# Low parts of the attention stage's weights: a subtraction on VectorE, or a negated copy on ScalarE and an accumulating DMA

## The chip, the core and the metric

The kernel runs on one core of a Trainium2 chip. The core has five instruction streams that run beside each other and meet only through semaphores: TensorE (PE in the profile) multiplies matrices, VectorE (DVE) and ScalarE (ACT) work elementwise, GpSimd (POOL) here clears small tiles and issues some DMAs, and SyncE (SP) issues most DMAs. Each stream executes strictly in its own order: an instruction that waits holds up everything behind it in that stream. The metric is the device time of one execution in microseconds (us); less is better.

## The reference

One layer of a decoder over 1024 tokens of width 1024, batch 1, in float32:

```python
h = rms_norm(x, attn_norm_w)
q, k, v, u, g = split(h @ w_in)                     # w_in: 1024 x 7168
a = rms_norm(diff_attention(q, k, v), subln_w)      # 8 heads, two softmaxes each, causal, shared bias
y_a = a @ w_proj_attn
c = silu(layer_norm(causal_depthwise_conv(u_a * sigmoid(u_b))))   # width 31
y_b = c @ w_proj_conv
g_a, g_b = split(sigmoid(g + gate_b))
x = x + (g_a * y_a + g_b * y_b) @ w_out
h = rms_norm(x, ffn_norm_w)
gt, up = split(h @ w_gate_up)
x = x + (silu(gt) * up) @ w_down
```

The inputs are float32, and the result is to keep close to float32 accuracy.

## The kernel before

TensorE multiplies in a fast format, float32r, which keeps fewer bits of the mantissa. To get the accuracy back, each operand is held as two tiles: a high part (`hi`, the value rounded to float32r) and a low part (`lo`, the value minus its high part). A product is then three matmuls, hi by hi, hi by lo and lo by hi (`mm3`, lines 159 to 162), all added up in one PSUM bank. Weights have to be split on the core, since they arrive from memory as plain float32.

**A weight fetch.** One fetch brings 512 KB of weights as a 128 x 1024 tile `wraw` (DMAs on SP's queue, line 287 in `ld_cols` for one fetch of 128 columns, line 308 in `ld_wide` for 512 rows of 256 columns). `wsplit` (line 276) then makes the two parts. ScalarE copies `wraw` to `whi` with rounding (`split_hi`, line 120), and VectorE subtracts `whi` from `wraw` into `wlo` (`split_lo`, line 125). There are two buffers for `wraw` and three each for `whi` and `wlo`. A `wraw` buffer can be loaded again once its subtraction is done. A `whi` or `wlo` buffer can be written again once the last matmul that reads it is done.

**The stream.** All weight fetches stand in one list (`Stream`, class `ws`). When a piece of work takes its next weights (`next`), the stream first starts new fetches until it holds three. So a fetch is begun while the two before it are still waiting to be used.

**The stages.** First the input norm and the projections of V, U and the first Q/K head, with convolution taps put between them on VectorE. Then attention, which interleaves three kinds of work: the 64 blocks of attention proper (8 heads by 8 row blocks), the rest of the input projection as filler (`later`: 7 Q/K items, 16 gate items, one to five per head), and the convolution taps that are left (`bg`). Then the two output projections, the merge, `w_out`, and the feed-forward layer.

**Attention.** For a head and a row block, `scores` (line 1009) multiplies on TensorE (lines 1022 and 1023, tile `sc`), adds the bias and takes the row extreme on VectorE (line 1024), takes the exponential on ScalarE (line 1029), and combines the two softmaxes on VectorE (line 1038). `turn` transposes the result on TensorE (line 1061, tile `pT`) and splits it into `ph` (ScalarE) and `pl` (VectorE); where a pair of row blocks is begun, POOL clears a corner of both (lines 1051 and 1052). `weigh` multiplies with V (tile `pW`), ScalarE copies the product out (`ar`, line 1075), and `back` transposes it and normalises (tiles `pB`, `an`, `jk`, lines 1081 to 1090). `subln_T` transposes a finished head (`pS`, `at`, lines 1102 to 1110). Filler items write PSUM tiles `pg`, which ScalarE takes out (`qkraw`, lines 756 to 759, for Q/K; `sgg`, line 603, for the gates). A finished Q/K item is transposed (`pQ`, line 774) and its parts are copied across partitions by DMAs on SP's queue (tiles `qs` and `ks`, lines 785 to 796).

**What sets the order.** The program is recorded by a framework that builds each engine's instruction stream from its own estimate of when each instruction would become ready; a few places pin the order by hand (`issue_after`). So an edit in one place changes the order of the streams around it. Waits and semaphores follow from which tiles are read and written.

**What the change touches.** `wsplit` alone, and only while the flag `inatt` is set. The flag is set at the start of attention and cleared after it; until now it only decided when the transposes of Q/K items are recorded. Thirty fetches are begun while it is set: twelve for Q/K heads 2 to 7, sixteen for the gates, and the first two of `w_proj_attn`. The feed-forward stage calls `wsplit` too, but with the flag cleared.

Of the kernel before, what the change touches and what calls it, by code (L numbers as in the profile page):

```python
# [12 lines left out]
AF = mybir.ActivationFunctionType  # L13
ALU = mybir.AluOpType
# [43 lines left out]
def kernel(  # L58
# [28 lines left out]
    dve, act, pool, pe = nc.vector, nc.scalar, nc.gpsimd, nc.tensor  # L87
# [24 lines left out]
    def nm(s):  # L112
        uid[0] += 1
        return f"{s}_{uid[0]}"

    def f32(ap):
        return ap.bitcast(F32)

    def split_hi(dst, src):
        act.copy(dst, src)  # L120
# [3 lines left out]
    def split_lo(dst, src, hi):  # L124
        last_lo[0] = dve.tensor_tensor(dst, src, f32(hi), op=ALU.subtract).ins  # L125
# [147 lines left out]
    def wtiles():  # L273
        return [wp.tile([P, 1024], F32R, tag=t_, name=nm(t_)) for t_ in ("whi", "wlo")]

    def wsplit(raw, tiles=wtiles):
        hi, lo = tiles()
        split_hi(hi[:], raw[:])
        split_lo(lo[:], raw[:], hi[:])
        return hi, lo  # L280

    def ld_cols(w, c0, tiles=wtiles):


        def go():
            raw = wraw()
            nc.sync.dma_start(
                raw[:].rearrange("p (k c) -> p k c", c=P),
                w[:, c0 : c0 + P].rearrange("(k p) c -> p k c", p=P),
            )  # L290
            hi, lo = wsplit(raw, tiles)
            return (
                hi[:].rearrange("p (k c) -> p k c", c=P),
                lo[:].rearrange("p (k c) -> p k c", c=P),
            )

        return [go]

    def ld_wide(w, cols):


        def half(g):
            def go():
                raw = wraw()
                r3 = raw[:].rearrange("p (k c) -> p k c", c=256)
                o = 0
                for c0, n in cols:
                    nc.sync.dma_start(
                        r3[:, :, o : o + n],
                        w[512 * g : 512 * (g + 1), c0 : c0 + n].rearrange(  # L310
                            "(k p) c -> p k c", p=P
                        ),
                    )
                    o += n
                hi, lo = wsplit(raw)
                return (
                    hi[:].rearrange("p (k c) -> p k c", c=256),
                    lo[:].rearrange("p (k c) -> p k c", c=256),
                )

            return go

        return [half(0), half(1)]
# [88 lines left out]
    def ld_pair(w, k, c):  # L412


        def go():
            raw = wraw()
            nc.sync.dma_start(
                raw[:].rearrange("p (k c) -> p k c", c=512),
                w[k * P : (k + 2) * P, 512 * c : 512 * (c + 1)].rearrange("(k p) c -> p k c", p=P),
            )  # L420
            hi, lo = wsplit(raw)
            return hi[:].rearrange("p (k c) -> p k c", c=512), lo[:].rearrange("p (k c) -> p k c", c=512)

        return go
# [378 lines left out]
                late.append((free if h else 0, lambda a_=(z, key, b, raw): turn_qk(*a_)))  # L803
            yield

    inatt = [False]
    MAKE = {"V": v_item, "U": u_item, "Q": q_item, "G": g_item}

    def run(items):
# [970 lines left out]
```

## Time and profile before

| quantity | value |
|---|---|
| median of 3 runs | 1759.88 us (1759.63 to 1760.11) |
| span of the profiled execution | 1756.3 us (no other time is listed for it) |
| median less span | 3.6 us |
| TensorE busy | 1743.5 us, 99% of the span |
| weight loads of TensorE (PEld) | 1501.9 us, 86% |
| VectorE busy | 1269.9 us, 72% |
| ScalarE busy | 807.5 us, 46% |
| GpSimd busy | 28.8 us, 2% |
| granted clock of TensorE | 1.000 |
| memory traffic | 175.55 MB read, 78.16 MB written |

The profile is one execution, taken by the hardware profiler. An engine is "busy" while an instruction executes; a wait is idle time in front of an instruction, put down to whatever released it last. Matmuls overlap their neighbours, so that a matmul's own duration (0.39 us for 512 columns) is longer than the distance to the next one; the distances are what TensorE's time is made of. Attention takes the span from 316 to about 842 us. "Landing" of a DMA is the time from its issue until its data are in place.

### The profile page before, as it was taken

To read this page: it belongs to the slowest core of one execution; us is meant where nothing else is said; L and a number is where in the kernel's file an instruction comes from. 1 tells how busy PE (TensorE), PEld (TensorE's weight loads), DVE (VectorE), ACT (ScalarE), POOL (GpSimd) and SP (SyncE) were. 2 spreads that over 40 slices of the span, in tenths; PEclk is the share of its full clock that TensorE was granted. 3 is DMA by queue.
4 is the path that set the end of the run, shared out by engine and by line. 5 is a ranking of instruction groups with operands and counts; after the bars stand their busy time and mean duration, and the time that the engine had idled before them with its cause. 6 is when DMAs were issued, how large, how long until landed. Compare 5 with 4: busy or idle time off the path is not lost.

```text
span 1756.3 us, 25881 instructions
## 1 busy us (share of the span) xinstructions
PE 1743.5 (99%) x9377; PEld 1501.9 (86%) x9377; DVE 1269.9 (72%) x2168; ACT 807.5 (46%) x1894; POOL 28.8 (2%) x107
## 2 busy tenths in 40 slices
PE   9999999999999999999999999999999999999999
PEld 7898998999998998988787888888888888888887
DVE  7388888998988988977777525876667666565544
ACT  5111341657776776765456313643333333333332
POOL 2001000000000000000000000000000000000000
PEclk9999999999999999999999999999999999999999
DMA  6237353234434444344872544235545544598663
GB/s 208 93 114 221 108 167 109 72 104 132 103 113 132 119 119 122 95 128 141 292 241 99 168 168 144 91 102 164 164 146 168 173 151 144 164 354 291 216 219 129
DMA packets 253156, 271.68 MB, mean 155 GB/s; under 512 B 15666, under 2 KB 177498, under 8 KB 253028
## 3 DMA queue, kind: packets, MB, share of 16 engines
q1 hardware_dynamic: 250848, 263.25, 47.0%
q0 software_dynamic: 1744, 5.19, 1.1%
q8 instruction: 74, 1.21, 0.3%
q10 hardware_dynamic: 436, 1.58, 0.2%
q14 instruction: 54, 0.44, 0.1%
HBM read 175.55 MB, written 78.16 MB: 144 GB/s over the span
## 4 chain that ended last, share of the span: by engine, by line
PE 92%; DMA 3%; DVE 2%; ACT 1%; issue 1%; SPq 0%; ACTq 0%; DVEq 0%
PE acc L1626 22%; PE pg L160 14%; PE pg L161 14%; PE pg L162 14%; PE acc L487 12%; PE sc L1023 2%; PE sc L1022 2%; PE pT L1061 2%; PE wo L162 2%; PE wo L160 2%; PE wo L161 2%; DMA gt<-g_d 1%; PE pW L160 1%; PE pW L161 1%; PE pW L162 1%; PE pg L848 1%
## 5 line engine op out<-in xcount | busy, mean ns | idle before, releaser
L565 DVE SCALAR_TENSOR_TENSOR acc<-u,cw,acc 128x1024 f32<-128x1024 f32 x240 | 307.1, 1280 | 2.7
L120 ACT CAST whi<-wraw 128x1024 fp32r<-128x1024 f32 x107 | 112.4, 1052 | 213.4 <-PE pg L161 129.1
L160 PE MATMUL pg<-hT_hi,whi 128*128 128x512 f32 x512 | 201.3, 393 | 0.0
L162 PE MATMUL pg<-hT_hi,wlo 128*128 128x512 f32 x512 | 201.1, 393 | 0.0
L161 PE MATMUL pg<-hT_lo,whi 128*128 128x512 f32 x512 | 200.9, 392 | 0.0
L160 PE MATMUL pg<-whi,hT_hi 128*128 128x256 f32 x704 | 200.3, 285 | 0.0
L162 PE MATMUL pg<-whi,hT_lo 128*128 128x256 f32 x704 | 200.2, 284 | 0.0
L161 PE MATMUL pg<-wlo,hT_hi 128*128 128x256 f32 x704 | 199.7, 284 | 0.0
L125 DVE TENSOR_TENSOR wlo<-wraw,whi 128x1024 fp32r<-128x1024 f32 x107 | 130.6, 1221 | 70.4 <-ACT whi L120 70.2
L125 DVE TENSOR_TENSOR wlo<-draw,whi 128x1024 fp32r<-128x1024 f32 x75 | 91.8, 1224 | 84.7 <-ACT whi L120 77.3
L120 ACT CAST whi<-draw 128x1024 fp32r<-128x1024 f32 x75 | 78.8, 1051 | 129.8 <-PE acc L487 116.3
L161 PEld LDWEIGHTS pg<-wlo,hT_hi 128*128 128x128 f32 x704 | 134.3, 191 | 1.9
L160 PEld LDWEIGHTS pg<-whi,hT_hi 128*128 128x128 f32 x704 | 134.1, 191 | 2.1
L162 PEld LDWEIGHTS pg<-whi,hT_lo 128*128 128x128 f32 x704 | 134.2, 191 | 1.4
L1029 ACT ACTIVATE E<-E,mn 128x640 f32<-128x640 f32 (+7 forms) x128 | 99.8, 780 | 46.4 <-DVE mn L1024 45.6
L487 PE MATMUL acc<-whi,wlo 128*128 128x512 f32 x308 | 119.8, 389 | 0.0
L487 PE MATMUL acc<-wlo,whi 128*128 128x512 f32 x308 | 119.8, 389 | 0.0
L162 PEld LDWEIGHTS pg<-hT_hi,wlo 128*128 128x128 f32 x512 | 96.2, 188 | 18.9
L161 PEld LDWEIGHTS pg<-hT_lo,whi 128*128 128x128 f32 x512 | 96.3, 188 | 18.8 <-issue 0.6
L160 PEld LDWEIGHTS pg<-hT_hi,whi 128*128 128x128 f32 x512 | 96.2, 188 | 18.9 <-issue 0.6
L1626 PE MATMUL acc<-h_lo,whi 128*128 128x512 f32 x240 | 93.4, 389 | 0.0
L1626 PE MATMUL acc<-h_hi,whi 128*128 128x512 f32 x240 | 93.4, 389 | 0.0
(295 smaller groups left out, 4030.0 us busy)
## 6 DMA issues: line engine op xcount, KB each, us to landing
wraw<-in_w_gate_up_dram SPq DMA_DIRECT2D x44, 512.0 KB, 4.6
wraw<-in_w_in_dram SPq DMA_DIRECT2D x40, 512.0 KB, 4.0
qs<-qs SPq DMA_DIRECT2D x96, 128.0 KB, 2.3
wd<-in_w_down_dram SPq DMA_DIRECT2D x44, 256.0 KB, 3.2
tdT<-wd SPq DMA_DIRECT2D x88, 128.0 KB, 4.4
draw<-sdS SPq DMA_DIRECT2D x44, 256.0 KB, 3.9
draw<-tdT SPq DMA_DIRECT2D x44, 256.0 KB, 3.9
wraw<-in_w_in_dram SPq DMA_DIRECT2D x32, 256.0 KB, 3.5
```

The source lines that it names most:

```text
L120: act.copy(dst, src)
L125: last_lo[0] = dve.tensor_tensor(dst, src, f32(hi), op=ALU.subtract).ins
L160: pe.matmul(o, lh, rh, start=start, stop=False)
L161: pe.matmul(o, lh, rl, start=False, stop=False)
L162: last_mm[0] = pe.matmul(o, ll, rh, start=False, stop=stop).ins
L487: m = pe.matmul(o[s_][i][:], l_[:, ts], r_[:, 512:], start=start and j + y_ == 0, stop=j == n - 1 and y_ == 2, skip_group_check=not start,)
L565: dve.scalar_tensor_tensor(acc[0][:], us[c][:, t : t + S], cw[:, c, t : t + 1], acc[0][:], op0=ALU.mult, op1=ALU.add)
L1022: pe.matmul(o[:, :w], qh[:, qs], k, start=True, stop=False)
L1023: last_mm[0] = pe.matmul(o[:, :w], ql[:, qs], k, start=False, stop=True).ins
L1029: act.activation(e[:, :nk], e[:, :nk], AF.Exp, bias=mn[:, j : j + 1], scale=-1.0, accum_out=l[:, j : j + 1])
L1061: pe.transpose(pt[:, k * P : (k + 1) * P], e[:, (k0 + k) * P : (k0 + k + 1) * P], ident[:])
L1626: pe.matmul(o[:], a_[x_][:, k, :], b_[y_][:, k, :], start=start and k + x_ + y_ == 0, stop=k == 3 and x_ == 1, skip_group_check=not start,)
```

## The change

For a fetch begun while `inatt` is set, VectorE no longer makes the low part. ScalarE writes the negated `wraw`, rounded to float32r, into `wlo`, which is the negated high part. Then POOL issues a DMA within SBUF that adds `wraw` to `wlo`, so that `wlo` holds `wraw` minus its high part. `whi` is made as before. The line that creates the flag moves up, so that `wsplit` can see it.

```diff
+    inatt = [False]
+
     def wsplit(raw, tiles=wtiles):
         hi, lo = tiles()
         split_hi(hi[:], raw[:])
+        if inatt[0]:
+            act.activation(lo[:], raw[:], AF.Copy, scale=-1.0)
+            pool.dma_start(f32(lo[:]), raw[:], accum_op=ALU.add)
+            return hi, lo
         split_lo(lo[:], raw[:], hi[:])
         return hi, lo
...
-    inatt = [False]
     MAKE = {"V": v_item, "U": u_item, "Q": q_item, "G": g_item}
```

## The prediction

> **What bounds the kernel now.** I read the page's busy times first, then the busy time by stage, then the waits of TensorE inside and just behind attention.
>
> ```profile
> span 1756.3 us, 25881 instructions
> PE 1743.5 (99%) x9377; PEld 1501.9 (86%) x9377; DVE 1269.9 (72%) x2168; ACT 807.5 (46%) x1894; POOL 28.8 (2%) x107
> 0.00:60.00 60.00, 56.10 (x342) 47.11 (x343) 36.69 (x84) 29.14 (x51) 11.70 (x27) 1.00 0.56 173
> 316.00:812.00 496.00, 496.00 (x3357) 456.50 (x3356) 436.92 (x1014) 345.34 (x1165) 10.90 (x61) 1.00 0.40 113
> 812.00:842.00 30.00, 28.43 (x156) 24.10 (x155) 20.89 (x40) 20.05 (x54) 0.93 (x5) 1.00 0.53 175
> 842.00:865.00 23.00, 20.97 (x95) 16.76 (x94) 14.15 (x24) 8.47 (x14) 0.00 (x0) 1.00 0.88 311
> PE pg L160 <- DVE gt L1354: 2.0, 1, 2.0
> PE pT L1061 <- ACT jk L1090: 1.5, 1, 1.5
> ```
>
> The stage rows read: start and end, length, then busy time of PE, PEld, DVE, ACT and POOL, the granted clock, DMA share and GB/s. The reader is to see that TensorE has no gap at all from 316 to 812 us, where nearly all of the edit lies, and that VectorE, though busy 436.92 of 496 us there (88%), is not what the time waits for. The last two rows are all that TensorE waits from 316 to 865 us. Since a matmul's end is modelled, busy alone could hide small gaps, so I also looked at the distances of starts.
>
> ```profile
> 439.84 0.39 PE L162 MATMUL pg<-hT_hi,wlo 128*128 128x512 f32 x1
> 440.06 0.39 PE L160 MATMUL pg<-hT_hi,whi 128*128 128x512 f32 x1
> ...
> 443.25 0.28 PE L160 MATMUL pW<-ph,vh 128*128 128x256 f32 x1
> 443.37 0.28 PE L161 MATMUL pW<-pl,vh 128*128 128x256 f32 x1
> ```
>
> A 512-column matmul follows the one before after 0.22 to 0.23 us, a 256-column one after 0.12 us, and so it goes on through attention: TensorE runs at its own pace. In the built order of the changed kernel the same matmuls stand in another sequence; with the trace's mean distance for each pair of neighbouring shapes, the stretch from the first to the last scores matmul adds up to 499.8 us, against 499.9 in the order before. The new order alone is worth nothing.
>
> **What the change can gain.** It takes 30 subtractions of 1.22 us off VectorE, 36.7 us.
>
> ```profile
> L125 DVE TENSOR_TENSOR wlo<-wraw,whi x29: 1207/1223/1229, 317.7 to 801.4; 128x1024 fp32r<-128x1024 f32 x29
> POOL pl L1052 <- PE pW L161: 247.2, 13, 45.3
> ```
>
> (29 lie ahead of 812 us, one at 825.77; the numbers are minimum, median and maximum in ns.) All lie beside a TensorE that is not waiting. So the most that can come back is the two waits, 1.5 + 2.0 = 3.5 us, with the 0.07 us that the stage rows show beside them, and neither names a subtraction: the first is held by ScalarE, the second by a gate product behind loads from memory. I take 0, and keep 0 to 3.6 us.
>
> **ScalarE.** Each of the 30 fetches adds a pass over 128 x 1024 elements. The nearest rows are the rounding copy and the exponential of the same size:
>
> ```profile
> 344.56 1.05 ACT L120 CAST whi<-wraw 128x1024 fp32r<-128x1024 f32 x1 [0.79 <-PE pg L162]
> 348.54 1.14 ACT L1029 ACTIVATE E<-E,mn 128x1024 f32<-128x1024 f32 x1
> 347.10 1.21 DVE L125 TENSOR_TENSOR wlo<-wraw,whi 128x1024 fp32r<-128x1024 f32 x1
> 358.60 0.39 PE L162 MATMUL pg<-hT_hi,wlo 128*128 128x512 f32 x1
> ```
>
> 30 x 1.05 to 1.14 is 31.5 to 34.2 us; I take 1.05, since it is also a copy with rounding. The number of activation-table loads in the program stays at seven. ScalarE goes from 345 to about 376 us busy of 496 (76%), still below what VectorE bears today. In front of TensorE this is worth nothing as long as every PSUM tile and every exponential has more than 1.05 us of room. It has none at one place, behind 812 us, where ScalarE's chain ends last already (the 1.5 us wait); in the new order two stretches there leave 0.2 and 0.3 us of TensorE work for a ScalarE copy and a VectorE split of 0.3 to 0.7 us. I take 0.6 us more than today.
>
> **POOL and the accumulating DMA.** Each fetch adds one issue on POOL and one DMA of 512 KB within SBUF. The trace has no accumulating DMA; the nearest rows are:
>
> ```profile
> L735 POOL DMA_DIRECT2D t_d<-b_d x8: 515/517/536, 144.6 to 148.1; - x8
> DMA to landing us min/median/max: 5.0/12.4/17.1
> 144.00:149.00 5.00, 5.00 (x24) 4.14 (x23) 4.89 (x6) 0.00 (x0) 4.09 (x8) 1.00 0.64 163
> qs<-qs SPq DMA_DIRECT2D x96, 128.0 KB, 2.3
> wraw<-in_w_in_dram SPq DMA_DIRECT2D x40, 512.0 KB, 4.0
> ```
>
> The first two rows are POOL's only large DMAs: 0.52 us to issue, and 5.0 us to landing for the fastest of eight that were issued back to back, 17.1 for the slowest, behind seven others of 576 KB. A copy within SBUF of 128 KB takes 2.3 us, a load of 512 KB 4.0. So the landing lies between 2.3 and 17.1 us, and a gain below the low end is excluded, since data must move. I take 6 us: near the 5.0 of the POOL row, as the new DMAs come one or two at a time, and a little more for the second operand.
>
> What it must beat is the time between the cast and the first use. The tightest tile is that of the four rows above: cast ended at 345.61, low part ready at 348.31, first used at 358.60. With the negated copy (1.05) and some 0.5 us until POOL issues, 358.60 - 345.61 - 1.55 = 11.4 us are left from issue to landing, and 6 fit. In the list of all 30, fourteen have between 11.4 and about 18 us (the last of them below), the other sixteen 26 or more.
>
> ```profile
> 824.68 1.06 ACT L120 CAST whi<-wraw 128x1024 fp32r<-128x1024 f32 x1
> 841.42 0.39 PE L162 MATMUL pg<-aTh,wlo 128*128 128x512 f32 x1
> ```
>
> The new order keeps this: between the matmul that frees the buffer and the first use of the new low part stand at least 17.3 us of TensorE work in all 30 cases, against 14.4 before at the tightest.
>
> **Queues.** On POOL the new issues stand among the clearings of `ph` and `pl`, whose waits for TensorE last up to 45.3 us. The built order puts each issue so that the instruction in front of it is free at least 17.6 us of TensorE work ahead of the low part's use, so POOL's order takes no more than the buffer itself does. What stands behind an issue is a clearing, late by the 0.52 us and by ScalarE's queue. On SP the load that refills `wraw` now waits for the accumulating DMA, and the copies of Q/K parts stand behind it:
>
> ```profile
> SPq L308 <- DVE wlo L125: 40.9, 5, 28.2
> L791 SPq DMA_DIRECT2D qs<-qs x28: 461/462/958, 380.8 to 786.6; - x28
> ```
>
> SP waits there today too. In the new order at least 20.3 us of TensorE work lie between the release of a low part's buffer and the first matmul that reads a copy queued behind such a load; 2.1 for the two ScalarE passes, 0.5, 6 and two copies of 2.3 make 13.2. Hidden, with 7 us to spare. The 30 x 512 KB add 15.7 MB read and as much written over 526 us, on DMA engines that are used at 0.40 to 0.53 there.
>
> **The sum.** 1756.3 (span) + 3.6 (what the median has beyond it) + 0 (order, VectorE, low parts) + 0.6 (ScalarE behind 812 us) = 1760.5 us.
>
> **A rule weighed.** The last row of the POOL fence shows eight issues at 0.51 to 0.54 us each while VectorE was busy 4.89 of 5.00 us. The Trainium skill, "SBUF — State Buffer", section "Who interferes with whom", says that VectorE and GpSimd share a port pair as an exclusive lock, so that a DMA issued from GpSimd waits for its descriptors while VectorE holds it. By that rule the issues would be late behind VectorE's work, which is the first rival; by this row they are not, at least beside convolution taps.
>
> **Rivals.**
>
> Low parts land late (slower). POOL's descriptors are held up, or the addition runs at a fraction of a copy's pace, and TensorE waits in front of a hi-by-lo matmul. It decides from a landing of about 11.4 us on. At 17.1 us the fourteen tight tiles, whose rooms average 15.8 us, miss by 5.7 us at the worst and by 20.7 us together: 1759.9 + 20.7 = 1781 us. For it: no row of an addition. Against it: POOL's issues of 0.52 us, 5.0 us for a single landing. Chance 0.13.
>
> ScalarE ends last (slower). Each negated copy stands in a strict queue ahead of exponentials and PSUM copies, and some are late by its 1.05 us. If a third of the 30 show, 10.5 us: 1770 us. For it: the one wait of TensorE in attention is on ScalarE. Against it: 29 casts of the same length stand in that queue today and none shows before 812 us. Chance 0.17.
>
> VectorE's relief reaches the end of attention (faster): both waits go, 1759.9 - 3.6 = 1756.3 us. Against it: neither is held by a subtraction, and the second lies behind loads. Chance 0.10, and in little over half of that the gain passes 0.2%.
>
> The edit runs but moves nothing that TensorE sees: this is my forecast, chance 0.60, between 1758 and 1763 us.
>
> **The numbers.** 0.2% is 3.5 us, about what a measurement of this kernel can tell from no change. Faster by more: 0.06. Slower by more: 0.13 + 0.17 + 0.02 of the forecast's upper edge = 0.32. Within: 0.62. The range takes in the ScalarE rival and the milder half of the late landings, 1756.5 to 1773 us, and leaves out the worse late landings and a full recovery of both waits.
>
> **What would show it.** Right: 30 fewer subtractions on VectorE and 30 ScalarE passes of 1.05 us by the line of the edit; TensorE still busy 496 of 496 us in attention; landing of the new DMAs below 11 us; no wait of TensorE named after them. Wrong: a wait of TensorE or of its weight loads on the DMA of `wlo`, many landings above 11 us, SP waits on those DMAs followed by waits for `qs` or `ks`, or TensorE waits on ScalarE spread through attention.

## The result and the profile after

The changed kernel takes 1768.65 us in the median (1767.41 to 1769.24), against 1759.76 us (1758.08 to 1760.11) beside it: a ratio of 1.0052, with an interval of 1.0040 to 1.0064. It is slower by about 9 us. The profiled execution spans 1767.5 us, 11.2 more than the one before. That is more than 9 us, since this is the longest of the four runs of the changed kernel (1769.24 us); the span before goes with the shortest of its kernel (1758.08 us), if the same 1.7 us lie between span and time.

The first lines of the page of the changed kernel:

```profile
span 1767.5 us, 25924 instructions
PE 1749.3 (99%) x9377; PEld 1504.9 (85%) x9377; DVE 1241.9 (70%) x2138; ACT 834.7 (47%) x1924; POOL 54.8 (3%) x137
```

Its busy time by stage, cut at the times used in the prediction (columns as there):

```profile
316.00:812.00 496.00, 490.77 (x3298) 451.06 (x3297) 399.96 (x960) 364.35 (x1175) 34.82 (x87) 0.99 0.55 141
812.00:842.00 30.00, 28.86 (x172) 24.84 (x171) 22.98 (x57) 19.81 (x59) 2.95 (x9) 1.00 0.50 140
```

The largest waits of TensorE between 250 and 960 us (in total, how often, the longest):

```profile
PE sc L1027 <- DMA ks<-klo: 2.7, 2, 1.9
PE sc L1027 <- DVE mn L1029: 2.3, 1, 2.3
PE pg L160 <- DVE gt L1359: 2.0, 1, 2.0
PE pg L161 <- DVE aTl L125: 1.0, 2, 0.8
```

TensorE, which had no gap before, is idle for 5.2 of the 496 us; the DMA engines went from 0.40 to 0.55. The first two waits are new, and neither names the low parts. They wait for `ks`, the key half of a Q/K item that a DMA on SP's queue copies across partitions, and for a VectorE pass that itself waits for a DMA (the bias tile `tb`). The new transfers, by the view of their tile (issue in ns: least, median, most):

```profile
L283 POOL DMA_DIRECT2D wlo<-wraw x30: 860/869/930, 318.3 to 835.0; - x30
DMA to landing us min/median/max: 4.4/5.2/7.8
```

SP's waits in front of the refill of `wraw`:

```profile
SPq L314 <- DMA wlo<-wraw: 99.1, 9, 23.7
SPq L293 <- DMA wlo<-wraw: 77.0, 16, 21.3
```

The DMA queues: POOL's queue (packets, MB, share of the time of all 16 DMA engines), and the median landing of the K copies:

```profile
q0 software_dynamic: 6064, 20.92, 5.8%
ks<-klo SPq DMA_DIRECT2D x32, 128.0 KB, 4.3
```

Before, the last two rows read:

```profile
q0 software_dynamic: 1744, 5.19, 1.1%
ks<-klo SPq DMA_DIRECT2D x32, 128.0 KB, 2.4
```

The accumulating DMAs land in time. What they cost shows elsewhere: the K copies take 4.3 us instead of 2.4, and SP stands in front of refill loads until an addition has landed.

**The first stall, at 704.9 us.** POOL's and SP's issues of the changed kernel in order of time (start, duration in us):

```profile
698.38 0.87 POOL L283 DMA_DIRECT2D wlo<-wraw  x1 [14.53 <-ACT wlo L282]
699.48 0.46 SPq L801 DMA_DIRECT2D ks<-klo  x1
699.99 1.51 SPq L802 DMA_DIRECT2D ks<-klo  x1
701.55 0.97 SPq L575 DMA_DIRECT2D c_d<-acc  x1
702.57 0.83 SPq L1006 DMA_DIRECT2D tb<-t_d  x1
```

The chain of waits across the stall (start, duration):

```profile
699.61 0.38 ACT ks L800
699.99 6.65 DMA ks<-klo
...
706.78 0.47 PE sc L1027
```

TensorE's instructions on either side of it:

```profile
704.65 0.28 PE L162 MATMUL pg<-whi,hT_lo 128*128 128x256 f32 x1
706.78 0.47 PE L1027 MATMUL sc<-ks,qs 128*128 128x512 f32 x1 [1.85 <-DMA ks<-klo]
```

And the windows around it:

```profile
704.00:707.00 3.00, 1.15 (x9) 0.97 (x9) 0.00 (x0) 0.61 (x4) 0.00 (x0) 1.00 0.94 317
707.00:712.00 5.00, 5.00 (x27) 4.77 (x27) 4.34 (x7) 1.93 (x6) 0.41 (x2) 0.66 0.36 114
```

An addition is issued at 698.38, two K copies right behind it. The second is issued at 699.99, behind ScalarE's pass for `ks` (line 800) and the issue before it on SP. That is 4.7 us before TensorE starts the last of its other matmuls, at 704.65. A copy of 2.4 us would fit, this one takes 6.65 us. The DMA engines are 0.94 busy there. The last row shows a second part of the price: behind the wait of 1.9 us the granted clock falls to 0.66 in the mean of 5 us. In the trace it stands at 0.50 for 3.4 of them (708.0 to 711.5 us), which costs 5.00 x (1 - 0.66) = 1.7 us more.

**The second stall, at 776 to 782 us.** The chain of waits:

```profile
769.08 0.95 ACT wlo L282
770.03 0.59 ACT ks L787
...
770.64 0.75 DVE klo L789
...
774.88 0.31 DVE E L1043
775.19 5.54 DMA tb<-t_d
...
780.90 0.69 DVE E L1029
```

SP's issues of the loads and K copies:

```profile
763.86 0.38 SPq L293 DMA_DIRECT2D wraw<-in_w_in_dram  x1
772.10 1.69 SPq L801 DMA_DIRECT2D ks<-klo  x1
773.84 1.30 SPq L802 DMA_DIRECT2D ks<-klo  x1
775.19 0.58 SPq L1006 DMA_DIRECT2D tb<-t_d  x1
```

The windows:

```profile
778.00:782.00 4.00, 1.70 (x8) 1.18 (x8) 1.10 (x3) 0.29 (x2) 0.00 (x0) 1.00 0.76 247
782.00:787.00 5.00, 5.00 (x17) 3.95 (x16) 3.32 (x11) 2.16 (x4) 0.00 (x0) 0.66 0.02 6
```

Here the refill load of `wraw` waited for an addition issued at 756.5 that landed 7.4 us later. So it ran beside the Q copies that stand behind it on SP's queue, and the four issued by 767 us landed in 4.0 to 4.3 us instead of 2.3. ScalarE's negated copy (0.95 us) stands ahead of the next K source. The next addition is issued at 770.3, and beside it the two K copies take 1.69 and 1.30 us to issue instead of about 0.5, and 3.9 us each to land. The bias load behind them starts at 775.19 and takes 5.5 us. TensorE idles 0.8 us for `ks` and 2.3 us for the pass that reads the bias, and then runs at half pace for a while.

Both stalls with their slow stretches make (1.9 + 1.7) + (0.8 + 2.3 + 1.7) = 8.4 of the 11.2 us between the profiled spans. The smaller waits nearly cancel: those on `aTl` and `sgg` (1.0 and 0.7 us) are new, and the 1.5 us on `jk` are gone. By the first lines of the two pages TensorE is also busy 5.8 us longer; 3.4 us of that are the two slow stretches, and the other 2.4 us are not explained by any run.

### The profile page after: what moved, and what is told of

The parts are those of the page before. It is cut to its first block, busy times and chain, and to the rows that moved or that the text cites. A ratio compares the mean times of both kernels' runs of the same rounds, so it can differ in the third digit from the quotient of the medians.

```text
span 1767.5 us, 25924 instructions
## 1 busy us (share of the span) xinstructions
PE 1749.3 (99%) x9377; PEld 1504.9 (85%) x9377; DVE 1241.9 (70%) x2138; ACT 834.7 (47%) x1924; POOL 54.8 (3%) x137
## 3 DMA queue, kind: packets, MB, share of 16 engines
q0 software_dynamic: 6064, 20.92, 5.8%
## 4 chain that ended last, share of the span: by engine, by line
PE 90%; DMA 4%; DVE 3%; ACT 2%; issue 1%; SPq 0%; DVEq 0%; ACTq 0%
PE acc L1631 22%; PE pg L160 13%; PE pg L161 13%; PE pg L162 13%; PE acc L493 12%; PE sc L1028 2%; PE sc L1027 2%; PE pT L1066 2%; PE wo L160 2%; PE wo L162 2%; PE wo L161 2%; DMA gt<-g_d 1%; PE pW L160 1%; PE pW L162 1%; PE pW L161 1%; PE pg L853 1%
## 5 line engine op out<-in xcount | busy, mean ns | idle before, releaser
L125 DVE TENSOR_TENSOR wlo<-wraw,whi 128x1024 fp32r<-128x1024 f32 x77 | 93.7, 1218 | 66.3 <-ACT whi L120 66.1
L1029 DVE CUSTOM_DVE_ANT_0 E<-sc,tb 128x512 f32<-128x512 f32 (+3 forms) x128 | 74.2, 585 | 34.7 <-PE pT L1066 13.3
```

The costliest lines, as they stand in the source:

```text
L1029: dve.tensor_tensor_reduce(e[:, ks], o[:, :w], tb[:, S - nk + c0 : S - nk + c0 + w], 1.0, mn[:, j : j + 1] if c0 else 3.0e38, ALU.add, ALU ...
```

## The experiments

The framework builds another order for the changed kernel, and an order can be worth something by itself. So all twelve kernels were run with the order held fixed. After recording, every instruction of each engine but those of the edit was tied behind its neighbour in a list taken from the built streams of the kernel before (the old order) or of the changed kernel (the new order):

```diff
+    for engine, places in ORDER.items():
+        ins = [i for i in recorded if i.engine == engine and i.name not in edited]
+        for a, b in zip(places, places[1:]):
+            tc.add_manual_dep(ins[b], ins[a].name, NoSync, reason="pinned order")
```

(The code is shortened.) Only the instructions that `wsplit` makes in attention are left free to find their place. The streams then differ in nothing else. The changed kernel itself is not pinned, but in the traces each engine of it runs the same instructions in the same sequence as in kernels 7 and 8, those of the edit included. The diffs below are against the changed kernel and leave out what marks these instructions as free. (The added code shifts line numbers: `scores` is at 1051 in most of these kernels, not at 1027.) Ratios are against the kernel before, run beside each; they take in all runs, so that the quotient of two medians can differ from them by up to 0.1%.

| kernel | order | work of a fetch in attention | us | ratio (interval) |
|---|---|---|---|---|
| changed | new | ScalarE negates, DMA adds | 1768.65 | 1.0052 (1.0040 to 1.0064) |
| 1 | new | VectorE subtracts | 1761.05 | 1.0010 (1.0002 to 1.0019) |
| 3 | new | ScalarE negates, VectorE adds | 1761.34 | 1.0017 (1.0008 to 1.0026) |
| 4 | new | VectorE negates, DMA adds | 1766.92 | 1.0041 (1.0027 to 1.0054) |
| 5 | new | VectorE subtracts, a DMA copy besides | 1761.52 | 1.0011 (1.0002 to 1.0020) |
| 9 | new | VectorE subtracts, a DMA addition besides | 1763.49 | 1.0022 (1.0013 to 1.0032) |
| 7 | new | ScalarE negates, DMA adds an eighth | 1761.43 | 1.0011 (1.0002 to 1.0020) |
| 8 | new | ScalarE negates, DMA copies | 1761.92 | 1.0015 (1.0006 to 1.0024) |
| 2 | old | ScalarE negates, DMA adds | 1778.78 | 1.0110 (1.0096 to 1.0124) |
| 6 | old | VectorE subtracts, a DMA copy besides | 1760.87 | 1.0010 (1.0001 to 1.0018) |
| 10 | old | VectorE subtracts, a DMA addition besides | 1765.28 | 1.0031 (1.0020 to 1.0041) |
| 11 | old | ScalarE negates, DMA copies | 1771.38 | 1.0058 (1.0046 to 1.0071) |
| 12 | old | ScalarE negates, VectorE adds | 1764.44 | 1.0030 (1.0019 to 1.0040) |

### 1. The new order alone

```diff
         if inatt[0]:
-            act.activation(lo[:], raw[:], AF.Copy, scale=-1.0)
-            pool.dma_start(f32(lo[:]), raw[:], accum_op=ALU.add)
+            split_lo(lo[:], raw[:], hi[:])
             return hi, lo
```

> The work of the kernel before (VectorE subtracts), but with every engine's stream pinned in the order that the changed kernel has; only the 30 subtractions find their own place. Three theories for the 8.9 us. Traffic: the accumulating DMAs slow the transfers beside them (the copies into ks land in 4.3 us instead of 2.4, the bias tiles in 4.9 instead of 3.7). Order: the new order alone brings copies and loads too near their use. ScalarE: the pass of 1.06 us ahead of the K copies makes them late. Traffic and ScalarE expect 1758 to 1762 us here, no wait of TensorE for ks at all, and landings of 2.4 us for ks; Order expects 1766 to 1770 us with the waits at 704 and 777 us still there. I hold Traffic the likeliest, so 1760 us.

1761.05 us, 1.0010. TensorE waits for no `ks` in attention; the K copies of this kernel there:

```profile
L825 SPq DMA_DIRECT2D ks<-klo x14: 461/468/547, 356.3 to 766.7; - x14
DMA to landing us min/median/max: 2.2/2.3/3.9
```

Traffic and ScalarE gave this, Order did not. The new order costs 0.1% (about 2 us, at the edge of the interval) and does not explain the rest.

### 2. The new work in the old order

The edit is the change itself, pinned in the old order.

> The work of the changed kernel (negated copy on ScalarE, accumulating DMA), with every engine's stream pinned in the order of the kernel before; only the 60 new instructions find their own place. Order expects 1758 to 1762 us. Traffic expects slower ks copies here too (4 us or more in the median) and 1762 to 1772 us, as far as the old order leaves less than 2 us of room at some of the 14 copies. ScalarE expects 1764 to 1772 us. SP's refill loads of wraw stand in the old places and wait for the accumulating DMA, so a delay behind them would show as waits of TensorE for qs or ks.

1778.78 us, 1.0110, worse than any theory gave. The waits of this kernel:

```profile
PE sc L1051 <- DMA ks<-klo: 7.6, 3, 3.7
SPq L317 <- DMA wlo<-wraw: 102.9, 17, 16.4
SPq L338 <- DMA wlo<-wraw: 91.9, 12, 24.1
```

The same wait, three times and longer. So the new order is not what makes the new work dear: with the new work it saves 10 us against the old one.

### 3 and 4. Half of the work each

```diff
             act.activation(lo[:], raw[:], AF.Copy, scale=-1.0)
-            pool.dma_start(f32(lo[:]), raw[:], accum_op=ALU.add)
+            dve.tensor_tensor(lo[:], raw[:], f32(lo[:]), op=ALU.add)
```

```diff
-            act.activation(lo[:], raw[:], AF.Copy, scale=-1.0)
+            dve.tensor_scalar(lo[:], raw[:], -1.0, None, op0=ALU.mult)
             pool.dma_start(f32(lo[:]), raw[:], accum_op=ALU.add)
```

> In the order of the changed kernel: the negated copy stays on ScalarE (30 passes of 1.06 us), but VectorE adds wraw to it (30 additions of about 1.22 us), so there is no accumulating DMA. Traffic expects 1758 to 1762 us, ks landing in 2.4 us. ScalarE expects 1765 to 1770 us. Order expects 1766 to 1770 us.

> In the order of the changed kernel: VectorE makes the negated copy (30 passes of 0.6 to 1.2 us), and the accumulating DMA stays, so ScalarE is relieved of its 30 passes. Traffic expects 1765 to 1770 us, ks landing in about 4.3 us and a wait of TensorE for ks of about 2 us near 704 us. ScalarE expects 1758 to 1762 us. Order expects 1766 to 1770 us.

With ScalarE's pass and no DMA 1.0017, which the intervals do not part from the order alone; with the DMA and no pass on ScalarE 1.0041. The DMA is the larger part. Traffic gave both times, and the wait of TensorE for `ks` (1.8 us in the fourth kernel), but not the landing of the K copies there: 3.2 us in the median, not 4.3. At 699 us the two K copies of the fourth kernel are slow again:

```profile
L825 SPq DMA_DIRECT2D ks<-klo x1: 1449/1449/1449, 699.2 to 699.2; - x1
L826 SPq DMA_DIRECT2D ks<-klo x1: 1184/1184/1184, 700.7 to 700.7; - x1
DMA to landing us min/median/max: 5.6/6.2/6.7
```

### 5 and 6. The transfer without the wait

```diff
-            act.activation(lo[:], raw[:], AF.Copy, scale=-1.0)
-            pool.dma_start(f32(lo[:]), raw[:], accum_op=ALU.add)
+            split_lo(lo[:], raw[:], hi[:])
+            pool.dma_start(f32(lo[:]), f32(lo[:]))
```

> The order of the changed kernel, VectorE's subtraction as before, and behind each of the 30 subtractions a POOL DMA of 512 KB that copies the finished low part onto itself. So the transfer is there, but the refill load of wraw on SP's queue does not wait for it (it waits for VectorE alone). Two theories are left for what the DMA does. Sharing: its 512 KB slow the copies into ks and the bias tile that run beside it; it expects 1765 to 1769 us here, a wait of TensorE for ks near 704 us, ks landings of 3 to 4.5 us. Held queue: SP stands at the refill load until the DMA has landed, and starts the load and the copies behind it late and together; it expects 1759 to 1762 us here, ks landing in 2.4 us, no wait for ks. I give Sharing 0.5 and Held queue 0.5.

> The same in the order of the kernel before: subtraction on VectorE, a copy of the low part onto itself by POOL's queue, and nothing on SP that waits for it. Against it stands the run of the changed work in this order, 1778.8 us. Sharing expects 1768 to 1780 us and waits of TensorE for ks. Held queue expects 1758 to 1762 us, no waits for ks.

1.0011 and 1.0010. A plain copy of the same 512 KB, for which SP does not wait, costs 0.1% in either order, in the new one no more than the order alone. In the old order one wait of 0.9 us for `ks` shows. "Sharing", as I had put it (512 KB beside the copies are enough), is refuted; "Held queue" is left standing by these two.

### 7 and 8. Less to add, or nothing to add

```diff
-            pool.dma_start(f32(lo[:]), raw[:], accum_op=ALU.add)
+            pool.dma_start(f32(lo[:, :128]), raw[:, :128], accum_op=ALU.add)
```

```diff
-            pool.dma_start(f32(lo[:]), raw[:], accum_op=ALU.add)
+            pool.dma_start(f32(lo[:]), raw[:])
```

> The order of the changed kernel and its work, but the accumulating DMA adds only the first 128 of the 1024 columns (64 KB; the other columns of the low parts stay the negated high parts). SP's refill still waits for it, for some 2 to 3 us instead of 5.2. Sharing expects 1760 to 1763 us (an eighth of the transfer; 1761.3 without any). Held queue expects 1763 to 1766 us, as about half of the wait is left.

> The order and the work of the changed kernel, but the DMA copies wraw into wlo and does not add (the low parts are then the weights themselves). If the addition makes the transfer slow, it lands well below 5.2 us (2.5 to 4) and the time falls to 1761 to 1765 us. If an addition costs no more than a copy, landing stays at about 5 us and the time at 1767 to 1770 us. I expect the second.

1761.43 and 1761.92 us. The seventh goes against "Held queue", which gave 1763 to 1766 us: SP's refills still wait for its DMA there (138 us in all). "Sharing" gave 1760 to 1763 us, but kernel 5 had gone against it. So neither theory holds by itself. My expectation of the eighth kernel was wrong. With a copy in the place of the addition, and with ScalarE's pass and SP's wait for the landing as in the changed kernel, the loss falls from 0.52% to 0.15%. Its transfers and its POOL queue:

```profile
L307 POOL DMA_DIRECT2D wlo<-wraw x30: 527/528/556, 317.9 to 826.7; - x30
DMA to landing us min/median/max: 2.8/3.3/8.3
q0 software_dynamic: 6064, 20.92, 3.4%
```

The bytes and packets, as the profile counts them, are those of the changed kernel (20.92 MB and 6064), the share of the DMA engines is not. The sequence of every engine's instructions is the same too, so the addition, and with it the values in the low parts, is all that the two kernels differ in. The 30 additions take (5.8% - 1.1%) of 1767.5 us, 83 us or 2.8 us each on all 16 engines (the 1.1% is what the same queue had before). The 30 copies take (3.4% - 1.1%) of 1759.8 us, 40 us or 1.3 us each. An addition occupies the engines twice as long as a copy of the same size, lands in 5.2 instead of 3.3 us, and takes POOL 0.87 instead of 0.53 us to issue.

### 9 to 12. The addition, the wait and ScalarE apart

Kernels 9 and 10 add the low part onto itself (`f32(lo[:]), f32(lo[:]), accum_op=ALU.add`) behind VectorE's subtraction, so that SP's refill does not wait for it. Kernel 11 is the eighth, kernel 12 the third, in the old order.

> The order of the changed kernel, VectorE's subtraction, and a POOL DMA of 512 KB that adds the finished low part onto itself (the low parts come out doubled). It is the run that copied the low part onto itself (1761.5 us), with an addition in place of the copy; SP's refill does not wait for it. Engines: the addition keeps the DMA engines busy twice as long as a copy (4.7% against 2.2% of the span of 16 engines, by the rows of the queue), and that alone slows the K copies; it expects 1765 to 1769 us, and the wait for ks near 704 us. Both: it takes the addition and the held refill together; it expects 1760 to 1764 us. I give Engines 0.6.

> The same addition onto itself in the order of the kernel before, nothing on SP waits for it. With a copy this was 1760.9 us, with the changed work 1778.8 us. Engines expects 1770 to 1780 us; Both expects 1760 to 1766 us.

> The order of the kernel before and the changed work, but the DMA copies wraw into wlo and does not add (the low parts are then the weights themselves); SP's refill waits for it. In the new order this was 1761.9 us. Engines expects 1760 to 1764 us here too. If the held queue is what costs in the old order, 1768 us or more, with waits of TensorE for ks; Both expects something between, 1762 to 1768 us.

> The order of the kernel before; ScalarE makes the negated copy and VectorE adds wraw to it, no DMA. It tells what of the 11.9 us of the copy with the held refill (1771.4 us) is ScalarE's pass and the low part's later finish by some 1 us, and what is the wait of SP's refill for a landing. If ScalarE's pass costs little in the old order too, 1760 to 1763 us and no wait for ks; if it is what makes the K copies late there, 1766 us or more with waits for ks. I expect the first.

1763.49, 1765.28, 1771.38 and 1764.44 us. "Engines" (the addition alone suffices) falls: kernels 9 and 10, without the wait of the refill, lose 0.2 and 0.3%, less than half of what the changed work loses in the new order and less than a third in the old one. "Both" holds for kernels 9 and 10; for 11 it gave at most 1768 us, too little. What came is the case named there for the held queue: 1768 us or more, and TensorE waits 3.0 us for `ks`. In the old order ScalarE's pass, a copy and the wait for it cost 0.58% together. The twelfth missed as well: ScalarE's pass costs 0.30% in the old order, where I expected at most 0.2%. It costs this in other places: TensorE waits 2.0 us more on ScalarE's `jk`, and never for `ks`.

In the old order the parts compare so: ScalarE's pass 0.30%; with a copy and the wait of the refill 0.58%; with an addition in its place 1.10%. In the new order the same row reads 0.17, 0.15 and 0.52%. (The pass and the wait are not parted by a kernel of their own in these last two steps.)

The wait is not the only thing that kernel 9 lacks. Its K copies are as slow as those of the changed kernel (4.3 us in the median, 7.3 at most), and yet TensorE waits only 0.2 us for them. Near 699 us its addition stands behind VectorE's subtraction and is issued at 699.49, after the first K copy; in the changed kernel it is issued at 698.38, ahead of both. So where an addition falls counts as well. Of the pairs that ran, 4 and 9 are the nearest for the wait alone (VectorE does the elementwise work in both): 1.0041 and 1.0022, with intervals that just overlap.

## Why the prediction was right, and where its reasons failed

The time lies in the range (1756.5 to 1773.0 us), but not in the forecast's own case: that said 1760.5 us and "moves nothing that TensorE sees", with 0.62 for no measurable change, and 0.52% with an interval of 0.40 to 0.64% is one. That the range holds the time is luck: its upper part was there for a ScalarE that ends last and for the milder late landings, and neither came about. What came is one of its own signs of being wrong, SP waits on the new DMAs followed by waits for `ks`. Step by step:

- **The order is worth nothing.** Nearly right: it costs 0.1%, about 2 us, at the edge of its interval (kernel 1). In the profiled execution of kernel 1, 1.7 of the 3.2 us by which its span exceeds that of the kernel before are a slow stretch of the clock, which need not come with the order (last section).
- **VectorE.** Right. Its subtractions of `wlo` from `wraw` fell from 107 to 77, and nothing came back for it: TensorE was not waiting for them.
- **ScalarE.** The duration was right (30 passes of 1.06 us, estimated 1.05). Its price is small in the new order (1.0017 against 1.0010, not parted by the intervals), near the 0.6 us estimated, but not where they were put: the 1.5 us wait on `jk` behind 812 us, to which they were to be added, is absent in the new order with the old work as with ScalarE's pass (kernels 1 and 3). The room was not as wide as I argued, as the old order shows (0.30%).
- **Landing and first use.** Right: estimated 6 us, measured 5.2 in the median and 7.8 at most, under the 11.4 of the tightest tile. No wait of TensorE names `wlo`. The rival in which low parts land late did not come about.
- **POOL's issue.** Mis-sized: 0.87 us, not 0.52. It had no consequence that the runs show. All thirty lie between 860 and 930 ns. The prediction took the rule that it weighed too widely. The section of the Trainium skill ("SBUF — State Buffer", "Who interferes with whom") names copy, cast and `tensor_scalar` as the operations of VectorE that can take the lock, and infers that a `tensor_tensor` does not hold up descriptors. The convolution taps of the row that the prediction set against the rule (the third of its POOL fence, not the last) are `scalar_tensor_tensor`. Beside a float32 `tensor_scalar` of 128 x 1024 the trace agrees with the rule: there the issue of an addition took up to 1.42 us instead of 0.87 (kernel 2, at 712.8 us), that of a copy up to 0.93 us instead of 0.53 (kernel 6, at 703.0 us), and the 930 ns above come from the one such case of the changed kernel. It is not the whole account, as kernel 4 has an issue of 1.17 us beside no such pass.
- **Queues: "Hidden, with 7 us to spare".** This is the step that failed. It took the room from the release of a low part's buffer to the first use of a copy, and 2.3 us for each copy. But the K copies do not start when the refill allows, they start when ScalarE and VectorE have made their sources, and some of them then have little more than their own landing left: at 704.65 us, 4.7 us for a copy of 2.4. (The pair of K copies at this place took up to 3.9 us in kernel 1, without a new DMA, 5.3 us in kernel 8, beside a copy, and 6.7 us here.) The six K copies between 694 and 782 us, beside additions, took 3.9 to 6.7 us. I had checked SP's order for what stands behind the refill, and not for what runs beside the DMA.
- **"On DMA engines that are used at 0.40 to 0.53".** A mean over 500 us said that there was room. In the 3 us of the first stall the share was 0.94. And the bytes were the wrong measure: I counted 15.7 MB read and written, as for a copy. The eighth kernel has the same bytes and loses 0.15% instead of 0.52%. The difference, 0.37% or 6.5 us, is the addition.

So the loss of about 9 us is, by the runs of the new order: about 2 us for the order (1.0010), about 1 us for ScalarE's pass, the wait for a landing and a copy's traffic together (1.0015 against 1.0010, within the intervals), and 6.5 us for an addition in place of a copy. Without SP's wait, with VectorE in ScalarE's place and with additions that are issued at other times, less is lost (1.0022); that it is the wait which is missing there is argued, not shown. How the addition's longer landing and its longer hold on the engines share in that is not settled: no kernel lengthened the one without the other.

## What to carry to other kernels

A DMA that adds is not a copy that happens to add: price it by the time that its packets take on the DMA engines, twice that of a copy here, and then look at what else is in flight in the same microseconds, not at the mean share of a stage. When a buffer is now released by a DMA instead of an engine, every queue entry behind its refill can move by a landing, and small transfers with a due time (here the K copies) can pay for it. Whether they do depends on the order: with a copy it cost nothing clear of noise in the new order, and 0.58%, ScalarE's pass included, in the old one. To tell an edit from the reordering that it causes, pin the order: the old and the new work in the old and the new order is four kernels, and here it showed that the new order, which looked suspect, was protecting the time.

## What the hardware showed that I had not expected

An accumulating DMA within SBUF of 128 x 1024 float32 takes 2.8 us of all 16 engines, a plain one 1.3 us, and its issue on POOL takes 0.87 us even for an eighth of the size (860 to 930 ns in the seventh kernel), against 0.53 us:

```profile
L307 POOL DMA_DIRECT2D wlo<-wraw x30: 860/869/930, 317.9 to 826.0; - x30
DMA to landing us min/median/max: 2.3/2.4/6.2
```

SP's own issues also became slower beside an addition: 1.3 to 1.7 us for a K copy whose issue takes 0.5 us otherwise. This is not peculiar to additions: with plain copies a K copy took up to 1.4 us to issue (kernel 5), and with no new DMA at all the issue of a bias load took 1.6 us (kernel 1). The Trainium skill, "DMA: Bandwidth & Descriptors", section "Queues, rings and completion order", says that each DMA engine takes turns between queues and switches only after a whole packet; that K copies on SP's queue slow down beside POOL's additions agrees with it (2.4 to 4.3 us), though no run here shows the packets themselves.

Gaps of TensorE can cost more than their length. After the waits of 1.9 us at 704.9 and 2.3 us at 779 us the granted clock was 0.66 over 5 us, each time with 3.4 us at 0.50 in it, so that 1.7 us were lost behind each. This does not follow every gap. A wait of 2.0 us on `gt`, behind attention, is in every trace. In the kernel before it lies between 862 and 868 us, and the clock stays at 1.00:

```profile
862.00:868.00 6.00, 3.98 (x17) 3.30 (x18) 5.28 (x8) 5.30 (x9) 0.00 (x0) 1.00 0.70 241
868.00:880.00 12.00, 12.00 (x54) 9.95 (x53) 12.00 (x21) 4.54 (x7) 0.00 (x0) 1.00 0.87 299
```

The same holds for the changed kernel and for nine of the twelve others. But in kernels 1, 5 and 6 the wait is followed by 3.4 us at 0.50 (in kernel 1 from 866.4 us). Two executions can thus differ by 1.7 us at a wait that they share.

The Trainium skill, "TensorE: Matmul & The Clock Gate", section "Part 1: The HAM clock gate", states that the clock halves after at least one idle window of about 3.4 us, and that the window runs freely. That it follows some gaps and not others agrees with a free-running window; the length does not, since 1.9 us were enough here, and in kernel 12 the 1.5 us on `jk` at 816 us.
